# One streaming layer on one core: two buffers for the convolution's input, and all nine gather buffers for 48 tokens of tile 6

## The chip, the cores and the metric

One core of a Trainium2 chip runs the whole program in one launch. The metric is device time in microseconds (us) of an execution, as the median of several runs. A profiled execution has, beside its time, a span (from its first instruction to its last), from which every row below is taken.

## What is computed

The reference is one layer on 1024 prompt frames and 32 sample frames of width 1024. Two recurrent mixers (gated linear attention and the gated delta rule) run in chunks over a projection of the normed input; before the second mixer stands a causal convolution of width 4 over 1536 channels. Then comes a product-key expert layer (PEER), and a last norm:

```python
proj = rms_norm(x, norm_mix_w) @ w_in
conv = silu(sum(conv_in[:, i:i + l] * gdn_conv_w[i] for i in range(4)))
q2 = l2_norm(cq) * 128 ** -0.5; k2 = l2_norm(ck)
x = x + concat([o1, o2]) @ w_out
# PEER: 8 heads, 128 x 128 keys, the 16 best experts of 16384 in each head
act = gelu(einsum('thkd,td->thk', peer_u[eidx], xblk))
x = x + einsum('thk,thkd->td', gate * act, peer_v[eidx])
y = rms_norm(x, norm_final_w)
```

A token thus needs 128 rows of `peer_u` and 128 rows of `peer_v`, 4 KB each.

## The kernel before

**Tiles.** The frames lie in eight tiles of 128 (0 to 7) and the sample's tile "S" of 32. `project` (L264) makes the projection of three groups of tiles: 0, 1, S; then 2, 3, 4; then 5, 6, 7. The mixers go through the tiles in order, and the second and third projection are woven into the steps of tiles 0 to 3 (`COMING`). Behind each group of tiles come the output projection, the routing (`route`, L493) and the choice of the best experts (`select`, L832).

**The convolution.** In `project`, block u of 128 channels is made by 24 matmuls (`by_channel`, L315) into one of two PSUM banks of the stream "pv" (in the second and third projection these two alone). For the 12 blocks of the convolution the bank is copied into a tile `ci` (L383), behind three old frames (L382). The convolution is one scaled copy on ACT (L390) and three multiply-adds on DVE (L392), all of which read `ci` and make `row`; then Silu on ACT (L394), whose table is loaded ahead of it, and behind it the mixers' table again (L102). For eight blocks the squares of `row` go into a tile `sq` (L401), whose sums PE makes one block later (`norms`, L356). `ci` has one buffer, and so has `sq` in the second and third projection (in the first, `sq` lies in another pool with three).

**PEER, two ways.** Tiles 2 to 5 (`DENSE`) are computed against all 16384 experts. `gate_matrix` (L932) writes their gates to DRAM; then `dense` (L994) runs over 128 blocks of 128 experts: eight times three matmuls `pD` (L194 to L196, a product of split numbers) and Gelu; the product with the gates `w*G` (L1010); a split into two parts; and, for each four blocks, 96 matmuls `pV`, whose eight banks DVE adds to `acc` (L1039). The other tiles (0, 1, S, 6, 7) gather their rows: `u_phase` (L1084) fetches for each slot one row of `peer_u` per token by an indirect DMA from POOL into `ug` (L1098) and multiplies and sums it on DVE (L1099). `v_phase` (L1113) fetches for each token its 128 rows of `peer_v` into `vg` (L1133); after each four tokens PE sums them by eight products (`pv`, L1139). This is called a visit below; tiles 0, 1, 6, 7 have 32 visits each and S has 8, so 136.

**Buffers of the gathers.** `vg` has five; `ug` has three in one pool and one in another. In `v_phase` the flag `more` lets a token whose place in a round of nine is 5 to 8 (`own >= VB`) use a buffer of `ug`.

**Order.** A scheduler sets each engine's order from the order in which the code was written, pools' free buffers and high priority (`urgent`, L1165, gives it to each step of `v_phase`). `weave` alternates between generators step by step. At the end of the code each gathered tile's `u_phase` is woven with the `v_phase` of the tile before it, and the last tile's `v_phase` stands alone. These are written behind `dense`, so their work fills what the rest leaves. The queues themselves run strictly in the order set.

```python
    prev = None
    for t in [t for g in GROUPS for t in g if t not in DENSE]:
        weave(values(prev, False) if prev is not None else None, u_phase(t, *sel[t]))
        prev = t
    weave(values(prev, True))
```

Of the kernel before, what the change touches and what calls it, by code (L numbers as in the profile page):

```python
# [11 lines left out]
F32 = mybir.dt.float32  # L12
# [9 lines left out]
P = 128  # L22
# [13 lines left out]
GROUPS = [[0], [1, "S"], [2, 3], [4, 5], [6, 7]]  # L36

DENSE = [2, 3, 4, 5]
# [20 lines left out]
VB = 5  # L59
NG = NT + 1 - len(DENSE)  # L60
WDB = 3
EARLY = [0, 1, "S"]

SP0 = 2
# [10 lines left out]
def layer_kernel(ctx: ExitStack, tc: tile.TileContext, A: dict):  # L75
# [24 lines left out]
    def mixer_tables():  # L100

        tc.keep_in_program_order(nc.scalar.preload_act_table_set("natural_log_exp_and_others"))  # L102
# [161 lines left out]
    def project(g):  # L264
# [60 lines left out]
        def row_tile():  # L325
            return p1.tile([P, 3 * P], F32, name="row", bufs=2)
# [40 lines left out]
        for u in range(16):  # L367
            p = by_channel(A["win_c"][u])
            if len(sqs) > (1 if first and u < 12 else 0):
                norms()  # L370
            if u < 4:
                row = row_tile()
                nc.scalar.activation(row[:, :N], p[:, :N], AF.Copy, scale=0.125 if u < 2 else 1.0)
                nc.sync.dma_start(d_qk[g][:, u, :], row[:, :N])
                yield None
                continue
            b = u - 4

            nf = N - DEC if sample else N
            L = N + 3 if sample else N  # L380
            ci = p1.tile([P, 3 * P + 3], F32, name="ci", bufs=1)
            nc.vector.tensor_copy(ci[:, 0:3], hist[:, b, :])  # L382
            nc.scalar.copy(ci[:, 3:3 + nf], p[:, :nf])  # L383
            nc.vector.tensor_copy(hist[:, b, :], ci[:, nf:nf + 3])
            if sample:
                nc.vector.tensor_copy(ci[:, nf + 3:nf + 6], tails[:, b, :])
                nc.scalar.copy(ci[:, nf + 6:L + 3], p[:, nf:N])
                nc.vector.tensor_copy(tails[:, b, :], ci[:, L:L + 3])
            row = row_tile()
            nc.scalar.activation(row[:, :L], ci[:, 0:L], AF.Copy, scale=cw[:, b, 0:1])  # L390
            for i in range(1, 4):
                nc.vector.scalar_tensor_tensor(row[:, :L], ci[:, i:i + L], cw[:, b, i:i + 1], row[:, :L],  # L392
                                               op0=ALU.mult, op1=ALU.add)
            nc.scalar.activation(row[:, :L], row[:, :L], AF.Silu)  # L394

            if not first:
                mixer_tables()
            if b < 8:
                sq = (rt.tile([P, 3 * P], F32, name="sq", tag="mixT", bufs=3) if first else
                      p1.tile([P, 3 * P], F32, name="sq", bufs=1))  # L400
                nc.scalar.activation(sq[:, :L], row[:, :L], AF.Square)  # L401
                sqs.append((b, sq))
            nc.sync.dma_start(d_cv[g][:, b, 0:nf], row[:, 0:nf])
            if sample:
                nc.sync.dma_start(d_cv[g][:, b, nf:], row[:, nf + 3:L])
            yield None
# [647 lines left out]
    def idx_of(ap):  # L1054
        return bass.IndirectOffsetOnAxis(ap=ap, axis=0)
# [28 lines left out]
    def u_phase(t, ei, eiT, gate):  # L1084

        act = gs.tile([P, P], F32, name="act", bufs=2)
        h2 = ge.tile([P, D], F32, name="h2", bufs=1)
        slots = DEC if t == "S" else P
        if t == "S":
            for c in range(4):  # L1090
                nc.sync.dma_start(h2[c * DEC:(c + 1) * DEC], h2d[t])
        else:
            nc.sync.dma_start(h2, h2d[t])
        yield None
        for k in range(slots):
            e = t == 0 or k % 4 < 3
            g = (ge if e else gp).tile([P, D], F32, name="ug", bufs=UB if e else 1)
            nc.gpsimd.indirect_dma_start(out=g, out_offset=None, in_=A["u"], in_offset=idx_of(ei[:, k:k + 1]))  # L1098
            nc.vector.scalar_tensor_tensor(g, g, 1.0, h2, op0=ALU.mult, op1=ALU.mult,  # L1099
                                           accum_out=act[:, k:k + 1])  # L1100
            yield None
        with tc.high_priority():
            nc.scalar.activation(act[:, :slots], act[:, :slots], AF.Gelu_apprx_tanh)
            if t in EARLY:
                mixer_tables()
            nc.vector.tensor_tensor(act[:, :slots], act[:, :slots], gate[:, :slots], op=ALU.mult)
            wT = gs.tile([P, P], F32, name="wT", bufs=2)
            pw = bank("pw", "pv")
            by_slot(pw, act, t)
            nc.scalar.copy(wT[:, :ntok(t)], pw[:, :ntok(t)])  # L1110
        ready[t] = eiT, wT

    def v_phase(t, more):  # L1113

        eiT, wT = ready[t]
        pv = [bank("pv0", "pv"), bank("pv1", "pv")]

        ns = ntok(t) // 4
        W4 = wT[:, :ntok(t)].rearrange("p (c r) -> p c r", c=4)
        for r in range(ns):  # L1120
            wd = gp.tile([P, 4, 32], F32, name="wd", bufs=WDB)
            nc.vector.scalar_tensor_tensor(wd, bc(iota128[:, None, :32], [P, 4, 32]), float(r),
                                           bc(W4[:, :, r:r + 1], [P, 4, 32]), op0=ALU.is_equal, op1=ALU.mult)
            vs = []
            for c in range(4):
                tok = c * ns + r

                own = (r * 4 + c) % (VB + UB + 1)
                if more and own >= VB:
                    g = (ge if own < VB + UB else gp).tile([P, D], F32, name="ug", bufs=UB if own < VB + UB else 1)  # L1130
                else:
                    g = gp.tile([P, D], F32, name="vg", bufs=VB)
                nc.gpsimd.indirect_dma_start(out=g, out_offset=None, in_=A["v"],  # L1133
                                             in_offset=idx_of(eiT[:, tok:tok + 1]))
                vs.append(g)
                yield None

            def product(half, c):
                return mm(pv[half][c * 32:(c + 1) * 32, :], wd[:, c, :], vs[c][:, half * 512:(half + 1) * 512],  # L1139
                          start=(r == 0), stop=(r == ns - 1), tile_position=(0, c * 32), skip_group_check=True)  # L1140

            with tc.issue_after(product(0, 3).ins):
                for half in range(2):
                    for c in range(3 + half):
                        product(half, c)
        x = gp.tile([P, D], F32, name="xf", tag="vg", bufs=VB)
        if t == "S":
            nc.gpsimd.memset(x, 0.0)
            for c in range(4):
                nc.sync.dma_start(x[c * 32:c * 32 + ns], xdram[t][c * ns:(c + 1) * ns])  # L1150
        else:
            nc.sync.dma_start(x, xdram[t])
        for half in range(2):
            cs = slice(half * 512, (half + 1) * 512)
            nc.vector.tensor_tensor(x[:, cs], x[:, cs], pv[half], op=ALU.add)
        nf = gp.tile([P, D], F32, name="nf", tag="vg", bufs=VB)
        load_nfin(nf)
        final_norm(x, gp, nf)
        if t == "S":
            for c in range(4):  # L1160
                nc.sync.dma_start(A["ys"][c * ns:(c + 1) * ns], x[c * 32:c * 32 + ns])
        else:
            nc.sync.dma_start(A["yp"][t * P:(t + 1) * P, :], x)
# [8 lines left out]
    def some(gen, n, pace=1):  # L1172

        while n is None or n > 0:
            for _ in range(pace):
                if next(gen, 0) == 0:
                    return
            n = n and n - 1
            yield None

    def values(t, more):
        return urgent(v_phase(t, more))

    def weave(*gens):
        gens = [g for g in gens if g is not None]
        while gens:
            for g in list(gens):
                if next(g, 0) == 0:
                    gens.remove(g)
# [3 lines left out]
    p1 = p1ctx.enter_context(tc.tile_pool(name="p1", bufs=1))  # L1193
# [5 lines left out]

    lmt = mc.tile([P, 6, P], BF16, name="lmt")  # L1200
    lm0 = mc.tile([P, P], BF16, name="lm0")
    lmw = p1.tile([P, 3 * P + 3], F32, name="lmw", tag="ci", bufs=1)[:, :P]
    lmu = mc.tile([P, 8, P], U8, name="lmu")
    nc.gpsimd.memset(lmt, 1.0)
    for i in range(7):
# [28 lines left out]
    sel, picked, mixT = {}, {}, {}  # L1234
# [54 lines left out]
    gctx.close()  # L1289
    dv = ctx.enter_context(tc.tile_pool(name="dv", bufs=1, side="right", reuse_waits="tile"))  # L1290
    dense(late)
    prev = None
    for t in [t for g in GROUPS for t in g if t not in DENSE]:
        weave(values(prev, False) if prev is not None else None, u_phase(t, *sel[t]))
        prev = t
    weave(values(prev, True))


OUTS = dict(yp=(SEQ, D), ys=(DEC, D), o_gla_p=(4, 64, 128), o_gdn_p=(4, 128, 128), o_conv_p=(128, 12, 3),
# [62 lines left out]
```

## Time and profile before

| | us |
|---|---|
| runs before: median (lowest to highest of 3) | 3216.44 (3214.72 to 3219.03) |
| profiled execution: its own time | 3227.73 |
| profiled execution: span | 3226.0 |
| PE busy, share of the span | 3045.9, 94% |
| DVE busy | 2293.4, 71% |
| POOL busy | 1319.6, 41% |
| ACT busy | 1260.6, 39% |
| DMA, mean over the span | 297 GB/s |

The shares are means over stages that have different limits; the stretches are read by themselves below. The last projection runs from about 490 to 690 us, the mixers, routing and choice of experts to about 1600, `dense` from 1577 to the end with the gathers beside it. PE's busy time is modelled, since its matmuls are pipelined; DMA shares are means over 16 engines.

### The profile page before, as it was taken

The page shows a single profiled execution, that of the slowest core. Times are in us where ns is not written, and L with a number is a line of the kernel's source. Part 1 is how long each engine was busy: PE and PEld are TensorE (multiplying, and loading weights), DVE is VectorE, ACT ScalarE, POOL GpSimd, SP SyncE. Part 2 cuts the span into 40 slices and gives each one's busy share as a digit, 9 for nine tenths or more (in the row PEclk, how much of TensorE's full clock was granted, in tenths as well). Part 3 has the DMA queues.
Part 4 walks back from the last instruction along what each step waited for, and adds up shares of the span by engine and source line. Part 5 has one row for each costly group of instructions (what it writes and reads, how often), then busy time and mean ns, then how long its engine had stood idle before and what let it go on. Part 6 is the DMA issues. An engine that isn't in the chain of part 4 may idle for free.

```text
span 3226.0 us, 49510 instructions
## 1 busy us (share of the span) xinstructions
PE 3045.9 (94%) x17739; PEld 2448.0 (76%) x17739; DVE 2293.4 (71%) x5691; ACT 1260.6 (39%) x2732; POOL 1319.6 (41%) x1181
## 2 busy tenths in 40 slices
PE   7999988799999989889799999999999999999998
PEld 7899977699877877778567777777777777777664
DVE  5557378888878999999977767767677667434333
ACT  6657345535332326788623223223222223223212
POOL 2100004343244545434455555555455555333444
PEclk9989998899999999999899999999999999999999
DMA  5632568888797989999998889989899899777988
GB/s 177 178 102 94 165 212 283 267 301 304 252 333 285 336 321 356 332 337 343 343 361 327 336 330 351 344 331 365 320 354 352 319 356 342 276 269 260 355 321 303
DMA packets 363977, 959.05 MB, mean 297 GB/s; under 512 B 35745, under 2 KB 137522, under 8 KB 359634
## 3 DMA queue, kind: packets, MB, share of 16 engines
q0 software_dynamic: 156672, 570.49, 48.3%
q1 hardware_dynamic: 141266, 351.84, 30.8%
q10 hardware_dynamic: 65792, 33.56, 3.6%
q8 instruction: 139, 2.28, 0.3%
q14 instruction: 108, 0.88, 0.1%
HBM read 893.00 MB, written 62.76 MB: 296 GB/s over the span
## 4 chain that ended last, share of the span: by engine, by line
PE 48%; DVE 1%; DMA 1%; issue 0%; ACT 0%; POOL 0%; POOLq 0%; DVEq 0%
PE pD L195 7%; PE pD L194 7%; PE pD L196 7%; PE pV L194 7%; PE pV L195 7%; PE pV L196 7%; PE pv L1139 6%; DMA vg<-v,eiT 1%; DVE ug L1099 0%; DVE vl L189 0%; DVE c L887 0%; DVE xf L1052 0%; POOL vg L1133 0%; ACT rs_junk L164 0%; DVE ul L189 0%
## 5 line engine op out<-in xcount | busy, mean ns | idle before, releaser
L1098 POOL DMA_INDIRECT ug<-u,ei x544 | 651.1, 1197 | 1143.1 <-DVE ug L1099 503.1
L1133 POOL DMA_INDIRECT vg<-v,eiT x488 | 579.0, 1186 | 595.2 <-PE pv L1139 438.1
L1099 DVE SCALAR_TENSOR_TENSOR ug<-ug,h 128x1024 f32<-128x1024 f32 x544 | 658.6, 1218 | 97.3 <-DMA ug<-u,ei 91.5
L194 PE MATMUL pD<-hh,uh 128*128 128x512 f32 x1024 | 402.8, 393 | 4.8 <-ACT uh L188 4.7
L195 PE MATMUL pD<-hh,ul 128*128 128x512 f32 x1024 | 403.1, 394 | 0.4 <-DVE ul L189 0.4
L196 PE MATMUL pD<-hl,uh 128*128 128x512 f32 x1024 | 402.6, 393 | 0.0
L195 PE MATMUL pV<-vh,wl 128*128 128x512 f32 x1024 | 400.9, 394 | 0.0
L196 PE MATMUL pV<-vl,wh 128*128 128x512 f32 x1024 | 398.5, 393 | 0.0
L194 PE MATMUL pV<-vh,wh 128*128 128x512 f32 x1024 | 378.6, 394 | 5.4 <-ACT wh L188 3.9
L188 ACT CAST vh<-vx 128x1024 fp32r<-128x1024 f32 x128 | 129.3, 1047 | 564.4 <-PE pV L195 397.5
L1039 DVE TENSOR_TENSOR acc<-acc,pV 128x512 f32<-128x512 f32 x248 | 163.9, 684 | 221.8 <-PE pV L196 195.4
L189 DVE TENSOR_TENSOR wl<-w,wh 128x512 fp32r<-128x512 f32 x302 | 207.7, 689 | 104.2 <-ACT wh L188 71.1
L188 ACT CAST wh<-w 128x512 fp32r<-128x512 f32 x302 | 186.1, 618 | 229.4 <-PE pcm L321 64.2
L1139 PE MATMUL pv<-vg,wd 128*32 128x512 f32 x1952 | 263.7, 614 | 8.7 <-DMA vg<-v,eiT 7.7
L991 ACT ACTIVATE w<-pD 128x512 f32<-128x512 f32 x128 | 76.6, 598 | 497.3 <-PE pD L196 458.3
L534 PE MATMUL pq<-h2T,wqb 128*128 128x256 f32 (+2 forms) x1280 | 248.7, 347 | 2.6 <-ACT gst L960 1.0
L194 PEld LDWEIGHTS pV<-vh,wh 128*128 128x128 f32 x1024 | 192.1, 188 | 65.6 <-issue 15.9
L195 PEld LDWEIGHTS pD<-hh,ul 128*128 128x128 f32 x1024 | 192.7, 188 | 60.4 <-issue 15.9
L194 PEld LDWEIGHTS pD<-hh,uh 128*128 128x128 f32 x1024 | 192.8, 188 | 58.4 <-issue 11.6
L196 PEld LDWEIGHTS pD<-hl,uh 128*128 128x128 f32 x1024 | 192.7, 188 | 55.9 <-issue 15.9
L195 PEld LDWEIGHTS pV<-vh,wl 128*128 128x128 f32 x1024 | 193.2, 189 | 54.5 <-issue 13.4
L534 PEld LDWEIGHTS pq<-h2T,wqb 128*128 128x128 f32 x1280 | 209.8, 193 | 26.0 <-issue 3.8
(339 smaller groups left out, 5433.8 us busy)
## 6 DMA issues: line engine op xcount, KB each, us to landing
ux<-ut SPq DMA_DIRECT2D x128, 512.0 KB
vx<-v SPq DMA_DIRECT2D x128, 512.0 KB
wqb<-wq SPq DMA_DIRECT2D x80, 576.0 KB
gd<-gst ACTq DMA_DIRECT2D x16, 2048.0 KB
G<-gd SPq DMA_DIRECT2D x32, 1024.0 KB
w<-win_c SPq DMA_DIRECT2D x96, 256.0 KB
wch<-wout SPq DMA_DIRECT2D x40, 512.0 KB
w<-win_t SPq DMA_DIRECT2D x72, 256.0 KB
```

The source lines that it names most:

```text
L188: nc.scalar.copy(hi, x)
L189: nc.vector.tensor_tensor(lo, x, hi.bitcast(F32), op=ALU.subtract)
L194: mm(out, a[0], b[0], start=first, stop=False, **kw)
L195: mm(out, a[1], b[0], start=False, stop=False, **kw)
L196: mm(out, a[0], b[1], start=False, stop=last, **kw)
L534: mm(p[:, :N], w[:, kb, :], h2T[:, kb, :], start=(kb == 0), stop=(kb == KB - 1))
L991: nc.scalar.activation(w, pD, AF.Gelu_apprx_tanh)
L1039: nc.vector.tensor_tensor(acc[ti][:, cs], before[:, cs], p, op=ALU.add)
L1098: nc.gpsimd.indirect_dma_start(out=g, out_offset=None, in_=A["u"], in_offset=idx_of(ei[:, k:k + 1]))
L1099: nc.vector.scalar_tensor_tensor(g, g, 1.0, h2, op0=ALU.mult, op1=ALU.mult, accum_out=act[:, k:k + 1])
L1133: nc.gpsimd.indirect_dma_start(out=g, out_offset=None, in_=A["v"], in_offset=idx_of(eiT[:, tok:tok + 1]))
L1139: return mm(pv[half][c * 32:(c + 1) * 32, :], wd[:, c, :], vs[c][:, half * 512:(half + 1) * 512], start=(r == 0), stop=(r == ns - 1), tile ...
```

## The change

`ci` gets a second buffer, and the squares are made in the block's own `ci`, which its multiply-adds have read by then; the single `sq` of the second and third projection goes. In the first projection the squares stay where they were. At the end of the code, `more` becomes a list that `v_phase` reads anew for each token: the last tile's `u_phase` is woven with 80 steps of tile 6's `v_phase` only; then `more` is set, and the other 48 tokens of tile 6 come by all nine buffers, as tile 7's do.

```diff
+SHARE = 80
...
-            ci = p1.tile([P, 3 * P + 3], F32, name="ci", bufs=1)
+            ci = p1.tile([P, 3 * P + 3], F32, name="ci", bufs=2)
...
                 sq = (rt.tile([P, 3 * P], F32, name="sq", tag="mixT", bufs=3) if first else
-                      p1.tile([P, 3 * P], F32, name="sq", bufs=1))
+                      ci[:, :3 * P])
...
-                if more and own >= VB:
+                if more[0] and own >= VB:
...
-    prev = None
-    for t in [t for g in GROUPS for t in g if t not in DENSE]:
-        weave(values(prev, False) if prev is not None else None, u_phase(t, *sel[t]))
-        prev = t
-    weave(values(prev, True))
+    gathered, more, sums = [t for g in GROUPS for t in g if t not in DENSE], [False], None
+    for t in gathered:
+
+        weave(some(sums, SHARE) if sums and t == gathered[-1] else sums, u_phase(t, *sel[t]))
+        if t == gathered[-1]:
+            more[0] = True
+            weave(sums)
+        sums = values(t, more)
+    weave(sums)
```

The scheduler takes up both parts, and the order of all engines changes from the first convolution block on. In the three places below the lines of the new kernel are two higher than those of the old one.

**ACT, one block of the last projection.** Before:

```order
L394 ACT_TABLE_LOAD
L394 ACTIVATE row<-row 128x384
L102 ACT_TABLE_LOAD
L383 COPY ci<-pcm 128x384
L401 ACTIVATE sq<-row 128x384
L390 ACTIVATE row<-ci,cw 128x384
```

And now:

```order
L385 COPY ci<-pcm 128x384
L392 ACTIVATE row<-ci,cw 128x384
L190 CAST wh<-w 128x512
L396 ACT_TABLE_LOAD
L396 ACTIVATE row<-row 128x384
L104 ACT_TABLE_LOAD
L403 ACTIVATE ci<-row 128x384
```

The copy out of the PSUM bank stood behind the Silu of the block before it and behind both table loads; now it stands ahead of them.

**DVE, where `dense` begins** (`w*G` is the first product that `pV` needs; the tiles `c` are buffers of `select`, here of tiles 6 and 7). Before, the first `w*G`:

```order
L899 COPY_PREDICATED c_14968<-c_14969,c_14968 128x128x2
L189 TENSOR_TENSOR ul<-ux,uh 128x1024
L1010 TENSOR_TENSOR w<-w,G 128x512
L899 COPY_PREDICATED c_14968<-c_14969,c_14968 128x128
L1010 TENSOR_TENSOR w<-w,G 128x512
L189 TENSOR_TENSOR wl<-w,wh 128x512
L1063 SCALAR_TENSOR_TENSOR c_12347<-c_14969 128x128
L1064 CAST ei<-c_12347 128x128
```

And now:

```order
L1012 TENSOR_TENSOR w<-w,G 128x512 x3
L900 TENSOR_SCALAR c_15070<-c_15070 128x128
L901 COPY_PREDICATED c_15069<-c_15070,c_15069 128x128x2
L191 TENSOR_TENSOR wl<-w,wh 128x512 x2
L901 COPY_PREDICATED c_15069<-c_15070,c_15069 128x128
L191 TENSOR_TENSOR wl<-w,wh 128x512
L1012 TENSOR_TENSOR w<-w,G 128x512
L1065 SCALAR_TENSOR_TENSOR c_12332<-c_15070 128x128
L1066 CAST ei<-c_12332 128x128
L191 TENSOR_TENSOR wl<-w,wh 128x512
L1074 CAST eiT<-pe 128x128
L1041 TENSOR_TENSOR acc<-xd,pV 128x512 x4
```

Before, the first `w*G` stood while tile 6's choice ended (`c_14969`) and tile 7's was still to come; now it stands where tile 7's choice ends (`c_15070`). Counted over the whole order, 260 products of gathered rows (L1099) stood ahead of the first `w*G`, and now 273; ahead of the first `acc` 264, and now 273. On PE 33 visits and 3 of the 128 blocks of `pD` stood ahead of the first `pV`, and now 36 and 4.

**DVE at the end of the program.** Before:

```order
L1039 TENSOR_TENSOR acc<-acc,pV 128x512 x2
L1052 SCALAR_TENSOR_TENSOR acc<-acc,rs_r,nfD 128x1024
L1155 TENSOR_TENSOR xf<-xf,pv_28032 128x512
L1155 TENSOR_TENSOR xf<-xf,pv_28033 128x512
L1052 SCALAR_TENSOR_TENSOR xf<-xf,rs_r,nf 128x1024
L1353 UNCONDITIONAL_BRANCH
```

And now:

```order
L191 TENSOR_TENSOR wl<-w,wh 128x512
L1041 TENSOR_TENSOR acc<-acc,pV 128x512 x5
L1054 SCALAR_TENSOR_TENSOR acc<-acc,rs_r,nfD 128x1024 x2
L1041 TENSOR_TENSOR acc<-acc,pV 128x512 x2
L1054 SCALAR_TENSOR_TENSOR acc<-acc,rs_r,nfD 128x1024
L1041 TENSOR_TENSOR acc<-acc,pV 128x512
L1054 SCALAR_TENSOR_TENSOR acc<-acc,rs_r,nfD 128x1024
L1359 UNCONDITIONAL_BRANCH
```

The last gathered tile's end (`xf`) stood last, and now the dense tiles' (`acc`) do. On PE the last two visits stood behind the last `pV`; now 212 matmuls `pD` and `pV` stand behind the last visit. On POOL 183 gathers of `peer_v` stood behind the last one of `peer_u`, and now 187; of all 544, 56 went to a buffer of `ug`, and now 77.

## Rows read from the trace of the kernel before

**Rows 1.** part 1 of the page: busy time, share of the span, instructions of each engine

```profile
PE 3045.9 (94%) x17739; PEld 2448.0 (76%) x17739; DVE 2293.4 (71%) x5691; ACT 1260.6 (39%) x2732; POOL 1319.6 (41%) x1181
```

**Rows 2.** windows: stretch, length; busy us (instructions) by engine; granted clock; DMA share, GB/s

```profile
1500.00:1600.00 100.00, 73.63 (x398) 58.27 (x396) 97.77 (x367) 67.06 (x177) 36.09 (x29) 0.85 0.97 333
1700.00:1800.00 100.00, 99.63 (x472) 75.20 (x472) 68.34 (x103) 27.82 (x36) 53.73 (x42) 1.00 0.85 318
2800.00:2900.00 100.00, 100.00 (x488) 72.60 (x487) 38.88 (x52) 24.75 (x32) 29.44 (x30) 1.00 0.75 264
3200.00:3226.00 26.00, 11.67 (x66) 4.62 (x65) 6.60 (x7) 4.31 (x12) 2.81 (x3) 0.70 0.58 228
```

**Rows 3.** timeline of PE from 2064.7: start us, us, what; 13 dense rows left out

```profile
2064.75 0.39 PE L195 MATMUL pV<-vh,wl 128*128 128x512 f32 x1
...
2067.96 0.39 PE L196 MATMUL pV<-vl,wh 128*128 128x512 f32 x1
2068.28 1.92 PE L1139 MATMUL pv<-vg,wd 128*32 128x512 f32 x16
2070.13 0.50 PE L195 MATMUL pD<-hh,ul 128*128 128x512 f32 x1
```

**Rows 4.** tiles pD and pV: ns min/median/max, first and last start

```profile
L194 PE MATMUL pD<-hh,uh x1024: 387/389/795, 1576.8 to 3176.0; 128*128 128x512 f32 x171
L196 PE MATMUL pV<-vl,wh x1024: 387/389/632, 1597.3 to 3205.8; 128*128 128x512 f32 x171
```

**Rows 5.** timeline of POOL, tile 6 alone: first of a four of gathers

```profile
2781.84 1.30 POOL L1133 DMA_INDIRECT vg<-v,eiT  x1 [8.76 <-PE pv L1139]
...
2944.38 0.94 POOL L1133 DMA_INDIRECT vg<-v,eiT  x1 [11.13 <-PE pD L195]
```

**Rows 6.** timeline of POOL, tile 7, nine buffers: first and last of the stretch

```profile
2989.84 1.00 POOL L1133 DMA_INDIRECT ug<-v,eiT  x1 [3.87 <-PE pv L1139]
...
3204.79 0.94 POOL L1133 DMA_INDIRECT vg<-v,eiT  x1 [0.30 <-issue]
```

**Rows 7.** timeline of all engines at the end

```profile
3206.10 0.62 PE L1139 MATMUL pv<-ug,wd 128*32 128x512 f32 x1
3206.21 0.69 DVE L1039 TENSOR_TENSOR acc<-acc,pV 128x512 f32<-128x512 f32 x1 [2.06 <-issue]
...
3209.99 0.33 SPq L1045 DMA_DIRECT2D yp<-acc  x1
...
3214.71 1.03 PE L1139 MATMUL pv<-vg,wd 128*32 128x512 f32 x1 [6.68 <-DMA vg<-v,eiT]
...
3222.20 0.33 SPq L1163 DMA_DIRECT2D yp<-xf  x1
```

**Rows 8.** waits from 515 to 690: who <- for whom: us, times, longest

```profile
PE pcm L321 <- ACT ci L383: 13.3, 5, 5.1
ACT wh L188 <- DMA w<-win_t: 19.3, 5, 8.6
ACT wh L188 <- DMA w<-win_c: 15.9, 5, 7.0
```

**Rows 9.** timeline of ACT and PE around 600

```profile
598.81 1.28 ACT L394 ACT_TABLE_LOAD   x1
...
600.65 1.28 ACT L102 ACT_TABLE_LOAD   x1
601.94 0.48 ACT L383 COPY ci<-pcm 128x384 f32<-128x384 f32 x1
602.48 1.01 PE L321 MATMUL pcm<-hh,wh 128*128 128x384 f32 x2 [5.10 <-ACT ci L383]
```

**Rows 10.** windows of the last projection

```profile
520.00:600.00 80.00, 63.03 (x349) 58.52 (x347) 69.64 (x167) 47.83 (x84) 32.11 (x28) 0.88 0.85 283
600.00:690.00 90.00, 79.49 (x531) 70.02 (x531) 77.35 (x189) 45.20 (x99) 35.95 (x31) 0.87 0.84 275
```

**Rows 11.** page, costliest groups: a gathered row's product on DVE

```profile
L1099 DVE SCALAR_TENSOR_TENSOR ug<-ug,h 128x1024 f32<-128x1024 f32 x544 | 658.6, 1218 | 97.3 <-DMA ug<-u,ei 91.5
```

More of the change, by code (lines that the diff above doesn't have):

```diff
@@ L1201, in layer_kernel @@
     lm0 = mc.tile([P, P], BF16, name="lm0")
-    lmw = p1.tile([P, 3 * P + 3], F32, name="lmw", tag="ci", bufs=1)[:, :P]
+    lmw = p1.tile([P, 3 * P + 3], F32, name="lmw", tag="ci", bufs=2)[:, :P]
     lmu = mc.tile([P, 8, P], U8, name="lmu")
```

## The prediction

> **What bounds the kernel now.** I read the page's busy times first, then windows to see in which stretch which engine is full, then the timelines of PE and POOL inside these stretches, and last the waits of the stretch in which the convolution is made. By the page PE is 94% busy, DVE 71%, POOL 41%, ACT 39% [rows 1]. These are means. The windows [rows 2] show two regimes. Up to about 1600 us DVE is the full engine (97.77 of 100 us from 1500 to 1600, PE 73.63). From 1700 on PE is (99.63, then 100.00 of 100 us, at a granted clock of 1.00), while DVE falls to 39.
>
> PE's busy time is modelled, so I check it by starts. From 2064.75 to 2067.96 fourteen dense matmuls start in a row, 3.21 us, so 0.229 us each; a visit (the sixteen small matmuls for four gathered tokens) starts at 2068.28 and the next dense matmul at 2070.13, so a visit costs 2.17 − 0.23 = 1.94 us [rows 3]. `dense` has 128 blocks of 24 `pD` and 24 `pV`, 6144 matmuls in all: 1407 us. Of 136 visits 33 stand ahead of the first `pV` and two behind the last, and the other 101 take 196 us. Together that is 1603 us of the 1629 between the first `pD` at 1576.8 [rows 4] and the last dense product's end, for which I take the visit behind it at 3206.10 [rows 7]. So 26 us at most are PE's idle time in there. **A gather that lands sooner shortens nothing in this stretch.** The change can act in three places only: at the very end, in the projections, and where `dense` begins.
>
> **Term 1, the end: −8.3 us.** While tile 6 has only five buffers, POOL issues four gathers and then waits for a visit to free buffers, 8.76 or 11.13 us at a time; twelve such fours take from 2781.84 to 2944.38, so 162.5 us for 48 gathers, 3.39 us each [rows 5]. Tile 7 with nine buffers takes 1.95 us each (110 intervals from 2989.84 to 3204.79) [rows 6]. The change gives tile 6's last 48 tokens the nine buffers, so the chain of gathers should end 48 × (3.39 − 1.95) = 69 us sooner. The DMA engines have room: share 0.75 in 2800 to 2900 [rows 2]. Now see what the gathers hold up [rows 7]. The last dense product is done by 3206; a visit follows there, and the last visit starts only at 3214.71, after 6.68 us for a gather; then come the last tile's end and its output at 3222.20, and the span ends at 3226.0, with PE's clock at 0.70 in that window [rows 2]. With 69 us gained, the visits are no longer last: the new order puts 212 dense matmuls behind the last visit, 212 × 0.229 = 48.5 us, which is well inside what the gathers gain. So the end becomes: 3206.1, plus the two visits that now lie inside `dense` (2 × 1.94 = 3.9), plus the dense tail from the last product to its output's issue (3209.99 − 3206.1 = 3.9), plus the output's landing, as at the end before (3226.0 − 3222.20 = 3.8). That is 3217.7, 8.3 us less than 3226.0. Bounds: 0 if the gathers gain under about 10 us and still end last, −10 if the dense tail takes half. What is late next is PE itself.
>
> **Term 2, the convolution's input: −8 us, between 0 and −27.5.** From 515 to 690 us PE waits five times, 13.3 us in all, for ACT to copy the bank into `ci`, since both banks are full [rows 8]. The longest wait is shown by ACT's timeline [rows 9]: the copy at 601.94 stands behind two table loads of 1.28 us and a Silu, and PE's matmul at 602.48 has waited 5.10 us. With two `ci` the copy stands ahead of them in ACT's order, so these 13.3 us can go. But PE idles 17.0 us in 520 to 600 and 10.5 in 600 to 690, 27.5 in all [rows 10], and the work behind the copies is bound elsewhere too: ACT's casts of the weights wait 19.3 and 15.9 us for DMAs [rows 8], and the DMA share is 0.84. Blocks that come sooner run into these. So one end is no gain at all, the other is all of the 27.5, and I take 8, some 60% of the 13.3 that the rows name. Whether it reaches the end depends on the stretch up to 1600, in which DVE is full. The gain is kept if DVE, too, gets its inputs sooner; it is at 70 and 77 of 80 and 90 us here [rows 10], so it has only about 23 us of slack itself. The squares in `ci` cost nothing by themselves: the same activation writes the same number of elements. They do add a wait, as a `ci` comes free only when PE has summed the squares. What stands behind that is DVE's copy of the old frames (L382) and DVE's row behind it; with two buffers it comes a block later, and I put it at 0, and at +5 us for the bound (five times a matmul's 1.01 us [rows 9]). Five more table loads on ACT (6.4 us) are covered by an engine that is 39% busy [rows 1]; without that cover they would cost these 6.4.
>
> **Term 3, where `dense` begins: +3 us, between 0 and +23.** The first `acc` now has nine more gathered products ahead of it on DVE (273 for 264), at 1.218 us [rows 11] 11.0 us; against that PE has three visits (3 × 1.94 = 5.8) and a block of `pD` (24 × 0.229 = 5.5) more ahead of its first `pV`, 11.3 us of useful work that is then not done later. These cancel but for the last rows of tile 7's choice; I take +3. All of it counts on PE only if PE runs dry, which it already nearly does there (26 us idle in 1500 to 1600 [rows 2]). The upper end is the second rival below. The order of tiles 0, 1 and S is otherwise the same, and 21 more gathers to buffers of `ug` (77 for 56) cost POOL nothing, as it waits most of its time.
>
> **Sum.** −8.3 − 8 + 3 = −13.3 us. The profiled execution took 3227.73 us (its span 3226.0 and 1.73 around it), so 3214.4 by that. It lies 11.3 us above the median of the runs, 3216.44, so I give the same difference from the median: **3203.1**. With the terms' nearer bounds (−3 to −14 for the second, 0 to +8 for the third) the forecast's own range is 3195 to 3212.
>
> **Rivals.**
> *Given back (0.22).* The 13.3 us of waits are replaced by waits for weights and DVE, so the second term is 0, and the start costs +8. For it: the 35.2 us for weights [rows 8] and a full DVE to 1600 [rows 2]. Against it: PE's waits for the copy are real, and ACT casts weights sooner in the new order. 3216.44 − 8.3 + 8 = 3216.1.
>
> *Slower: the first `w*G` comes late (0.14).* In DVE's new order the first `w*G` stands where tile 7's choice ends, no longer tile 6's. 13 more products (260 to 273) are 15.9 us [rows 11], and tile 7's choice on a full DVE is about as much again, an estimate from the same stretch: 34 us. PE has 11.3 us of visits and `pD` to fill it; the rest, 23 us, is idle time ahead of the first `pV`. With no gain in the projections: −8.3 + 23 = +14.7, 3231.1. It decides if PE idles over some 15 us more between 1500 and 1660 than now. Against it: a place in the order is not a time, and DVE may reach it sooner.
>
> *All of the projection's idle time goes (0.12).* 27.5 us, and the granted clock of 0.88 and 0.87 there [rows 10] rises with PE's work. −8.3 − 27.5 + 3 = −32.8, so 3183.6.
>
> *The gathers, not PE, set the end (0.03).* Then PE has slack inside `dense`, and the chain's 69 us come off whole, or near it: 3216.44 − 69 = 3147.4. The starts speak against it: 1603 of 1629 us are accounted for by matmuls at their closest spacing. The Trainium skill (Perfetto Trace Analysis, section Identifying the Most-Contended Engine) warns that the share of time in which matmuls are busy is no good measure, since they are pipelined, and would have one look at the share of weight loads. That share is 76% here [rows 1], so by that rule a quarter of PE would be free, and this rival the forecast; the spacing of 0.229 us shows that it is not.
>
> The likeliest case, the sum above, has the remaining 0.49.
>
> **How the numbers follow.** I count 0.2%, 6.4 us, as what a measurement of this kernel can tell: faster is below 3210.0, slower above 3222.9. Faster: the third and fourth rival and most of the forecast, 0.12 + 0.03 + 0.45 = 0.60. Same: the first rival and the forecast's upper edge, 0.22 + 0.03 = 0.25. Slower: the second rival and 0.01, 0.15. The range goes from 3183 (the projection's whole gain) to 3226 (half of the late start), which leaves out the fourth rival, part of the third and most of the second, about 0.2.
>
> **What would show it.** Term 1: the last gathers of tile 6 about 1.95 us apart; the last visit some 48 us ahead of the last `pV`; the issue of `acc`'s output as the last row of the end, with no visit waiting for a DMA behind the last `pV`. Term 2: the wait of `pcm` for the copy gone between 515 and 690, and less PE idle time in its two windows; if the wait is gone and the idle time is not, the first rival holds. Term 3: the first `pD` and `pV` (1576.8 and 1597.3 [rows 4]) move earlier by the second term's gain, less 3 us. The prediction is wrong if PE idles over 15 us more in 1500 to 1660 than before, if the gathers of tile 6 don't speed up, or if `dense` from its first `pD` to its last `pV` takes anything but its 1629 us plus the two visits and what the start adds.

## The result, and the profile after

| | us |
|---|---|
| kernel before: median (4 runs; the range) | 3215.64 (3214.72 to 3219.03) |
| changed kernel: median (4 runs; the range) | 3248.31 (3239.80 to 3252.63) |
| ratio, 95% interval | 1.0093 (1.0078 to 1.0108) |
| changed kernel, profiled execution: time, span | 3239.80, 3238.1 |

The change makes the kernel 33 us slower between the medians, 12.1 us between the two profiled spans (3226.0 and 3238.1). The forecast was 3203.1, and its range ended at 3226. The profiled execution of before (3227.73) lies 12.1 us above its median, that of the changed kernel 8.5 below; a second profile of the changed kernel, below, has a span of 3249.1 and the same shape.

Part 1 of the changed kernel's page differs little from [rows 1]: no engine has much more to do.

```profile
PE 3034.5 (94%) x17739; PEld 2445.8 (76%) x17739; DVE 2290.1 (71%) x5691; ACT 1267.4 (39%) x2737; POOL 1323.4 (41%) x1181
```

Windows of the changed kernel (columns as in [rows 2]): the stretch where `dense` begins, and the end.

```profile
1500.00:1600.00 100.00, 73.67 (x406) 59.52 (x404) 88.42 (x276) 74.69 (x193) 40.81 (x32) 0.80 0.89 302
1600.00:1700.00 100.00, 70.24 (x320) 50.85 (x321) 70.82 (x156) 29.35 (x47) 50.78 (x41) 0.83 0.94 351
1700.00:1800.00 100.00, 100.00 (x475) 75.49 (x474) 68.18 (x102) 27.18 (x35) 49.57 (x41) 1.00 0.93 335
3200.00:3226.00 26.00, 26.00 (x116) 21.45 (x116) 10.18 (x14) 6.91 (x14) 0.00 (x0) 1.00 0.04 15
```

Before, for 1600 to 1700:

```profile
1600.00:1700.00 100.00, 92.38 (x413) 68.46 (x413) 76.19 (x143) 29.93 (x47) 52.72 (x43) 0.97 0.92 348
```

From 1700 on PE is full as before. **Most of the loss is in one place**: between 1600 and 1700 PE is busy for 70.24 us where it was 92.38, 22.1 us less, at a granted clock of 0.83. The waits of PE from 1500 to 1700 (who, for whom: us, times, longest), first before, then of the changed kernel, say what it waits for:

```profile
PE pw L1082 <- DVE act L1106: 11.6, 1, 11.6
PE pgm L959 <- ACT gA L956: 8.5, 10, 1.5
...
PE pV L194 <- ACT wh L188: 3.9, 2, 2.1
```

```profile
PE pgm L961 <- ACT gA L958: 24.3, 13, 8.9
PE pV L196 <- ACT wh L190: 18.8, 2, 18.6
PE pv L1141 <- DMA vg<-v,eiT: 12.0, 1, 12.0
```

`pV` waits 18.6 us for `wh`, which is cast from the first `w*G`. So the first `w*G` is late. To see why, follow it back through timelines and lists of tiles. Before, the last write of the gates to DRAM (ACT's queue), the loads of `G` and the one ahead of them (SP's), the first `w*G` (DVE) and the first `pV` (PE):

```profile
1556.28 0.52 ACTq L962 DMA_DIRECT2D gd<-gst  x1
```

```profile
1575.67 0.30 SPq L1091 DMA_DIRECT2D h<-h2d_S  x1
1576.07 1.01 SPq L1000 DMA_DIRECT2D G<-gd  x2
```

```profile
1590.03 0.67 DVE L1010 TENSOR_TENSOR w<-w,G 128x512 f32<-128x512 f32 x1
```

```profile
1596.11 1.09 PE L194 MATMUL pV<-vh,wh 128*128 128x512 f32 x4
```

And in the changed kernel:

```profile
1598.42 0.52 ACTq L964 DMA_DIRECT2D gd<-gst  x1
```

```profile
1619.69 0.80 SPq L1002 DMA_DIRECT2D G<-gd  x2
```

```profile
1631.81 1.28 DVE L1012 TENSOR_TENSOR w<-w,G 128x512 f32<-128x512 f32 x2
```

```profile
1633.20 1.22 PE L196 MATMUL pV<-vh,wh 128*128 128x512 f32 x2 [18.62 <-ACT wh L190]
```

From the write's issue to the load of `G` it is 19.8 us before and 21.3 now; from there to the first `w*G` 14.0 and 12.1. So from the last gate's write to the first `w*G` it takes 33.8 and 33.4 us: the same. What moved is the write itself, by 42.1 us, and everything behind it moved with it: the first `w*G` by 41.8, the first `pV` by 37.1 (1596.1 to 1633.2). So the choice of tile 7, which now stands between that write and the first `w*G` and which the prediction's second rival feared, costs nothing there.

The Trainium skill (DMA: Bandwidth & Descriptors, section Anatomy of one DMA) gives a transfer 2.0 us and its bytes at 436 GB/s; it fits that to another path of issue than this one. For the write's 2048 KB that would be an estimate of 6.8 us. The rows show 19.8 and 21.3 between the write's issue and the load of `G`, with the DMA engines 0.89 to 0.97 busy: a price read off the Trainium skill would miss two thirds of this. In the changed kernel the load waits for the write itself. Before, it stands behind a load of `h` on SP's queue, which comes at 1575.67; in the profile of `e2` below, with the same order there, the wait of that load is put down to a write of the gates.

The gates are late because DVE does other work first. The last `gA` (a DVE product of the gate matrices, shown by the tile's list) starts at 1551.5 before and at 1589.1 now:

```profile
L953 DVE TENSOR_TENSOR gA<-iota,gmf x128: 666/681/689, 1226.0 to 1551.5; 128x512 f32<-128x512 f32 x128
```

```profile
L955 DVE TENSOR_TENSOR gA<-iota,gmf x128: 664/680/730, 1237.1 to 1589.1; 128x512 f32<-128x512 f32 x128
```

DVE's busy time up to that start, of the gathered products alone (two records a product) and of the tiles `c` alone, on which the routing and the choice work (windows by line and by tile; behind the length, DVE's busy time is the first column of the first row, the third of the second), before and then now:

```profile
0.00:1551.50 1551.50, 307.89 (x504) 0.95 0.77 263
...
0.00:1551.50 1551.50, 0.88 (x10) 0.49 (x10) 308.23 (x1770) 49.01 (x160) 0.95 0.77 263
```

```profile
0.00:1589.10 1589.10, 323.84 (x530) 0.94 0.78 265
...
0.00:1589.10 1589.10, 0.82 (x10) 0.50 (x10) 324.06 (x1905) 55.15 (x177) 0.94 0.78 265
```

13 more products (504 to 530 records) are 15.95 us, 135 more records on `c` (22 of them the routing's, the others the choice's) 15.83: 31.8 of the 37.6 us by which the last `gA` moved. Counted over the order, 252 products stood ahead of the last `gA`, and now 265; of tile 6's choice nothing did, and now nearly all of it does. The gates stand behind them in DVE's queue. The Trainium skill (PSUM — Partial Sum Buffer, section Engine vs sequencer instructions) calls these queues strict FIFO; these rows agree.

DVE is not slower, it does its work in another order: up to 1589.1 it is busy for 1283.78 us before and 1284.23 now. What comes sooner is the last routing, and tile 6's choice behind it. The last of its products `psc` on PE starts 38.4 us earlier:

```profile
L546 PE MATMUL psc<-wqb,qb x256: 270/275/527, 416.8 to 1533.6; 128*128 128x128 f32 x128
```

```profile
L548 PE MATMUL psc<-wqb,qb x256: 273/275/377, 419.9 to 1495.2; 128*128 128x128 f32 x128
```

In the projection the wait did go, and others took its place. PE's waits from 515 to 690 now (for before [rows 8]):

```profile
PE pga L632 <- DVE kh L627: 10.0, 4, 3.8
PE pga L632 <- DVE att L642: 4.7, 3, 2.6
PE pgs L656 <- DVE mix L680: 3.8, 1, 3.8
PE pcm L323 <- ACT ci L385: 3.2, 2, 2.6
```

`pcm` waits 3.2 us for the copy where it waited 13.3. But PE then stands behind the mixer's DVE steps (`kh`, `mix`), and the last matmul of the last projection starts at 658.1, later than before (653.4):

```profile
L321 PE MATMUL pcm<-hh,wl x408: 289/337/689, 20.4 to 653.4; 128*128 128x384 f32 x90, 128*128 128x288 f32 x46
```

```profile
L323 PE MATMUL pcm<-hh,wl x408: 289/337/525, 20.5 to 658.1; 128*128 128x384 f32 x90, 128*128 128x288 f32 x46
```

PE's busy time from 500 to 700 is 165.28 us, 4.4 less than the 169.66 of before.

At the end the first term of the prediction can be read off. The last visit stands at 3180.0, ahead of the last `pV`; the last rows of DVE are `acc`:

```profile
3180.04 0.59 PE L1141 MATMUL pv<-vg,wd 128*32 128x512 f32 x1
...
3230.04 0.39 PE L198 MATMUL pV<-vl,wh 128*128 128x512 f32 x1
```

```profile
3230.46 0.69 DVE L1041 TENSOR_TENSOR acc<-acc,pV 128x512 f32<-128x512 f32 x1 [0.83 <-PE pV L198]
3232.93 1.28 DVE L1054 SCALAR_TENSOR_TENSOR acc<-acc,rs_r,nfD 128x1024 f32<-128x1024 f32 x1 [1.78 <-ACT rs_r L172]
```

From the last `pV` to the span's end it is 8.1 us (3230.0 to 3238.1); before it was 20.2 (3205.8 to 3226.0). Less the two visits that now lie inside `dense` (3.9), that is 8.2 us gained.

### The profile page after: what moved, and what is told of

It reads as the page before. It is cut to its first block, busy times and chain, and to the rows that moved or that the text cites. A ratio compares the mean times of both kernels' runs of the same rounds, so it can differ in the third digit from the quotient of the medians.

```text
span 3238.1 us, 49519 instructions
## 1 busy us (share of the span) xinstructions
PE 3034.5 (94%) x17739; PEld 2445.8 (76%) x17739; DVE 2290.1 (71%) x5691; ACT 1267.4 (39%) x2737; POOL 1323.4 (41%) x1181
## 4 chain that ended last, share of the span: by engine, by line
PE 50%; DMA 5%; DVE 4%; ACT 2%; issue 1%; POOL 0%; ACTq 0%; DVEq 0%
PE pV L196 7%; PE pV L198 7%; PE pV L197 7%; PE pD L197 7%; PE pD L198 7%; PE pD L196 7%; PE pv L1141 6%; DMA gd<-gst 5%; PE pgm L961 1%; DVE ug L1101 1%; DVE gA L955 1%; DVE gB L953 1%; ACT gA L958 1%; PE pq L536 0%; ACT gst L962 0%
## 5 line engine op out<-in xcount | busy, mean ns | idle before, releaser
L1135 POOL DMA_INDIRECT vg<-v,eiT x467 | 566.1, 1212 | 476.6 <-PE pv L1141 336.3
L1141 PE MATMUL pv<-vg,wd 128*32 128x512 f32 x1868 | 256.0, 602 | 13.8 <-DMA vg<-v,eiT 13.7
L198 PEld LDWEIGHTS pV<-vl,wh 128*128 128x128 f32 x1024 | 192.4, 188 | 54.5 <-issue 13.4
```

Source lines behind the costliest of these rows:

```text
L198: mm(out, a[0], b[1], start=False, stop=last, **kw)
```

## The experiments

Twelve experiments, four on each of three chips. The kernel before stood at 3217.67 (21 runs), 3232.33 (23) and 3230.71 us (35) on them, so ratios to its runs on the same chip are compared, not times. **Theory G** (late gates): the convolution's part changes the order, DVE does products and choice ahead of the last gate matrices, and `dense` starts late. **Rival P**: the projection itself lost the time. **Rival S**: the faster gathers disturb `dense`. Where a row is shown, it is one tile's list: times of one (min/median/max, ns), first and last start.

### First chip: the parts alone, and the gates put first

`e1_ci_only` is the kernel before with the first part of the change:

```diff
-            ci = p1.tile([P, 3 * P + 3], F32, name="ci", bufs=1)
+            ci = p1.tile([P, 3 * P + 3], F32, name="ci", bufs=2)
...
-                      p1.tile([P, 3 * P], F32, name="sq", bufs=1))
+                      ci[:, :3 * P])
```

> Only the convolution's part: two ci, squares in ci; the end of the program as before. Theory G (late gates): the whole loss comes from this part, because the order it brings puts more of DVE's other work ahead of the last gate matrix. Then the last write of the gates is issued at about 1598 us (before 1556.3), the first pV starts at 1633 within 6 us (before 1596.1), and the time is 3245 to 3258, at or a little above the changed kernel's 3248. Rival P (the projection itself lost the time, its clock being 0.83 in 600 to 700 where it was 0.89): also slow, but the first write of the gates and all after it are late by one constant amount, some 14 us, not by a growing one. Rival S (the faster gathers at the end disturb dense): this kernel is at 3216 or below.

Measured: 3244.28 us, 1.0072 (1.0051 to 1.0093).

```profile
L962 ACTq DMA_DIRECT2D gd<-gst x16: 520/521/578, 1269.1 to 1605.3; - x16
```

```profile
L194 PE MATMUL pV<-vh,wh x1024: 387/389/796, 1641.0 to 3238.5; 128*128 128x512 f32 x171
```

The loss is all here. The time is a microsecond below what was expected. Beside `e2` on the same chip (below) the first gate write is 22.6 us late (1246.5 there), the last 54.0 (1551.3): it grows, which speaks against P's constant amount as the whole cause. S falls.

`e2_share_only` is the second part alone (the diff above, without the lines on `ci` and `sq`).

> Only the end: 48 tokens of tile 6 by nine buffers; the convolution as before. Theory G: everything up to dense as before (last write of the gates 1556, first pV 1596, each within 4 us); the last visit lies ahead of the last pV, and the end saves what the prediction's first term says, 8 us: 3205 to 3211, 0.9965 to 0.9985 of before. Rival S: slower than before by 10 us or more, with dense matmuls further apart than 0.229 us where the gathers are faster.

Measured: 3212.44 us, 0.9980 (0.9966 to 0.9994), 5.2 us faster.

```profile
L964 ACTq DMA_DIRECT2D gd<-gst x16: 520/521/577, 1246.5 to 1551.3; - x16
```

```profile
L1141 PE MATMUL pv<-vg,wd x1868: 592/592/1063, 895.5 to 3177.5; 128*32 128x512 f32 x187
```

```profile
L196 PE MATMUL pV<-vh,wh x1024: 387/389/628, 1590.9 to 3203.4; 128*128 128x512 f32 x171
```

The front is that of before (5 us early), the last visit lies ahead of the last `pV`, the time is just above the range expected.

`e3_gates_first` is the whole change, and the gates in the helper `urgent`:

```diff
-    gms = chain(*(gate_matrix(t) for t in GORD[:GN]))
+    gms = urgent(chain(*(gate_matrix(t) for t in GORD[:GN])))
...
-    weave(selecting(), chain(gms, *(gate_matrix(t) for t in GORD[GN:])),
+    weave(selecting(), urgent(chain(gms, *(gate_matrix(t) for t in GORD[GN:]))),
```

> The change whole, and beside it high priority for each step of the gate matrices (the helper urgent, as v_phase has it); nothing else. Theory G: the last write of the gates comes back to 1550 to 1570, the first w*G to 1585 to 1605, the first pV to 1590 to 1610, and the time to 3200 to 3218. Rival P: the priority does not touch the projection, so the time stays above 3235. Rival S: the same, above 3235.

Measured: 3222.44 us, 1.0010 (0.9994 to 1.0026), a little above the range expected.

```profile
L964 ACTq DMA_DIRECT2D gd<-gst x16: 520/520/578, 1260.1 to 1558.8; - x16
```

```profile
L196 PE MATMUL pV<-vh,wh x1024: 387/389/504, 1602.3 to 3218.2; 128*128 128x512 f32 x171
```

With both buffers and the gates early again, `dense` begins 34 us sooner (1636.7 in the run below, on the same chip, to 1602.3) and 24 us are back. P falls as the main cause, as the convolution is still the changed one. But 10 us remain to the end alone, and the projection's own share is not nothing: its last matmul starts at 655.8 here and at 649.6 in `e2`.

`after_again` is the changed kernel once more.

> The changed kernel a second time, as its first profile explains only 12 of the 33 us between the medians. Theory G: again the last write of the gates at 1598 within 8 us and the first pV at 1633 within 8 us; 3240 to 3253. If the two executions differ by 10 us, the stretch in which they part (windows of 100 us) is to show whether it is the gates' stretch or another.

Measured: 3246.13 us, 1.0074 (1.0052 to 1.0096), span 3249.1; last gate write 1599.3, first `pV` 1636.7. Of the 11.0 us between its span and the first profile's, 3.5 are at the first `pV`; the rest comes inside `dense`, where PE waits longer for casts of `w` and `u`: its waits from 1700 on are, for `wh` and `uh`,

```profile
PE pV L196 <- ACT wh L190: 4.3, 3, 3.3
PE pD L196 <- ACT uh L190: 4.0, 2, 2.4
```

where the first profile has 1.2 and 2.6.

This run and `e2` differ in the convolution alone, on one chip. Between their profiles the last `gA` moves from 1546.1 to 1590.0, 43.9 us. Up to it DVE is busy for 1248.1 and 1284.7 us, so 36.6 of the 43.9 are work that now comes first; the other 7.3 are idle time of DVE, 6.9 of it ahead of 700, and that is what is left for P.

### Second chip: other ways to late gates

`e4_sq_only` has the squares in the block's `ci`, of which there is still one (the second pair of lines of `e1`'s diff). The other half, two `ci` beside the old `sq`, was not tried: the kernel's tiles leave no room for it.

> Before, and only the squares made in the block's ci, which keeps its one buffer. In its order 263 gathered products stand on DVE ahead of the last gate matrix (252 before, 265 with both buffers) and tile 7's whole choice ahead of the first w*G. Theory G (late gates cost the time, not the second buffer as such): the last write of the gates comes 25 to 45 us later than before's 1556, the first pV 25 to 45 later than 1596, and the time is 3235 to 3255. Theory B (the second buffer is what brings the late order): within 5 us of before, 3212 to 3222, with the gates at 1556.

Measured: 3277.21 us, 1.0140 (1.0107 to 1.0174), 45 us slower and more than expected. `e7`, whose order up to `dense` is that of before, gives the same chip's front: last gate write 1568.3, first `pV` 1608.0. Here:

```profile
L962 ACTq DMA_DIRECT2D gd<-gst x16: 520/521/4440, 1281.6 to 1628.8; - x16
```

```profile
L194 PE MATMUL pV<-vh,wh x1024: 387/389/794, 1672.1 to 3266.8; 128*128 128x512 f32 x171
```

60.5 and 64.1 us late. Theory B falls: the squares' place brings a late order without the second buffer. With a single `ci` the projection is late as well: in 515 to 690 PE waits 9.2 us for the squares it is to sum, the projection's last matmul starts at 683.5 (`e7` 650.4), and the gates' first write is 26 us late (1281.6; `e7` 1255.6). So these 45 us are not the gates' order alone.

`e6_late_gates` is the kernel before, with a lower priority for the last gates alone (`later` is `urgent` with a negative offset):

```diff
-    weave(selecting(), chain(gms, *(gate_matrix(t) for t in GORD[GN:])),
+    weave(selecting(), later(chain(gms, *(gate_matrix(t) for t in GORD[GN:])), 1500),
```

> Before, and only a lower priority for the gate matrices that are still open when the last choice begins, so that 61 more instructions of the choice and 4 more gathered products stand on DVE ahead of the last one; convolution and end as before. Theory G: the last write of the gates 12 to 25 us later than 1556, the first pV later by about as much, PE gets one block of pD and one visit done ahead of it (7.4 us), and the time goes up by what is left, 5 to 18 us: 3222 to 3236. If the gates' place does not decide, within 4 us of before.

Measured: 3257.58 us, 1.0088 (1.0064 to 1.0113).

```profile
L962 ACTq DMA_DIRECT2D gd<-gst x16: 520/521/2500, 1254.8 to 1593.1; - x16
```

```profile
L194 PE MATMUL pV<-vh,wh x1024: 387/389/793, 1636.0 to 3236.0; 128*128 128x512 f32 x171
```

This shows the last step by itself: with the old convolution and the old end, gates that are 24.8 us late (1568.3 in `e7` to 1593.1) and a first `pV` 28.0 us late (1608.0 to 1636.0) cost 25 us between the medians. Of the 24.8, 12.5 are at the last `gA` (1563.6 and 1576.1), the rest at the steps behind it, which have the lower priority too. The size is above the 5 to 18 expected: the first `pV` came later than the 12 to 25 us thought of, 28.0 less the 7.4 of work done ahead is 20.6, and 25 were measured.

`e5_share_gates` has the second part of the change and `e3`'s two lines.

> Only the end of the program (48 tokens by nine buffers) and high priority for the gate matrices; the convolution as before. The first experiment on the gates with the whole change stood 10 us above the end alone. Theory G with a gain that is given back (the two ci bring nothing to the gates): this kernel is at 3203 to 3213, at or below the end alone (3212), and 8 to 18 below the whole change with gates first (3222). Rival: the priority itself costs those 10 us by moving other work behind the gates; then this kernel is at 3217 to 3226.

Measured: 3237.24 us, 1.0021 (1.0002 to 1.0040). This missed: it is no faster than before. As a ratio it lies where the rival put it, that the priority itself costs those 10 us (3217 to 3226 is up to 1.0026 on the first chip). `e7_share_24` is the end with `SHARE = 104`.

> The end alone, with 24 tokens of tile 6 by nine buffers for 48 (SHARE 104). By the prediction's first term the gain is that the visits no longer come last, not the gathers' speed: half the tokens gain 35 us on the gathers, still more than the 15 that are wanted, so the time is that of 48 tokens, 3208 to 3216. If the gathers' own time counted, half the gain would be lost: 3215 to 3217 or, against before, 0 to -3 us.

Measured: 3235.13 us, 1.0007 (0.9989 to 1.0024). Not the gain of 48 tokens, but on another chip.

### Third chip: the end and the gates side by side

`e8_share_48`, `e9_share_24b`, `e10_share_gates_b` and `e11_whole_gates_b` are `e2`, `e7`, `e5` and `e3`.

> The end alone, 48 tokens, again, beside the next three on one chip, since the first eight runs lay on two chips, on which before stood at 3218 and at 3232. Theory G: 0.9965 to 0.999 of before, as the first time (0.998). If the gain of the first time was the chip's, 0.999 to 1.002.

> The end alone with 24 tokens, again. If only the place of the last visits counts, the same ratio as with 48 tokens, to within 0.0015. If the gathers' gain itself counts, higher than with 48 tokens by 0.002 or more.

> The end, and high priority for the gate matrices, the convolution as before; again. If the priority itself costs something, because the first w*G then stands behind 18 more instructions of the choice (1320 for 1302), this is above the end alone by 0.001 to 0.004; if not, within 0.001 of it.

> The whole change with gates first, again. Against the kernel before it in this call it has the two ci alone. If the two ci bring nothing to the end once the gates are early: within 0.0015 of it. If they bring the prediction's 8 us: 0.0025 below it. If they cost something of their own beside the gates: 0.0025 or more above it.

| | us | ratio (95%) |
|---|---|---|
| `e8`: end, 48 tokens | 3220.73 | 0.9967 (0.9951 to 0.9984) |
| `e9`: end, 24 tokens | 3225.81 | 0.9986 (0.9968 to 1.0004) |
| `e10`: end, gates first | 3232.29 | 1.0006 (0.9989 to 1.0023) |
| `e11`: whole change, gates first | 3235.17 | 1.0020 (1.0000 to 1.0040) |

The end alone gains on this chip too. 24 tokens lie between 48 and none here, and at 1.0007, no gain, on the second chip; the intervals overlap, so how much of the gain needs the second 24 stays open. In the profile of `e9` PE is held up once more, between 2920 and 2940, at a clock of 0.91:

```profile
2920.00:2940.00 20.00, 18.02 (x80) 12.70 (x79) 11.67 (x16) 10.98 (x16) 8.21 (x7) 0.91 0.94 344
```

`e10` stands 0.0039 above `e8`: the priority itself costs 11.6 us. (Not by the 18 more instructions of the choice that were expected: by the records of the traces 9 fewer of `select` stand ahead of its first `w*G` than in `e8`.) Its gates are written 4.7 us sooner than `e8`'s (1556.8 and 1561.5), and yet the first `pD` starts later, 1589.8 for 1582.0, and the first `pV` with it (1606.3 for 1602.4). The longest wait (PE's waits from 1500 to 1610):

```profile
PE pw L1084 <- DVE act L1108: 13.8, 1, 13.8
```

`pw` stands ahead of the first `pD` on PE and waits for a gathered tile's last products, which the gates were put before; it starts at 1584.9; in `e8` its wait is 11.6 and it starts at 1572.5. So with the gates early the next thing that is late is that. It explains the first `pD`; of the 8.0 us between the two spans 3.9 are at the first `pV`, and the other 4.1 come inside `dense`, from a cause that stays open. `e11` stands 0.0014 above `e10`, within the 0.0015: the two `ci` bring nothing that shows once the gates are early. The intervals leave no room for a gain of 8 us, but some for a loss of as much.

## Why the prediction was wrong

- **Term 1, the end, −8.3 us: right.** 8.2 by the profile of the changed kernel; alone, −5.2 and −10.0 us between medians on two chips. The reason was right (the last visits move into `dense`). Its supporting number was too good: from the first of tile 6's last 48 gathers (2764.74) to the first of tile 7's (2888.39) POOL takes 123.7 us, 2.6 each, not 1.95. Before, it took 160.6 (2771.64 to 2932.23), so the gathers gained 37 us, not 69, which was still enough. POOL goes on waiting for the visits that free the buffers, 7.37 us for one at 2888.39. In the whole change this gain is no help on top: in `e1` the late `dense` ends behind the last visit (3234.9) already.
- **Term 2, the convolution, −8 us: wrong, it is 0 at best.** The step that failed is from "the wait goes" to "PE gets further". The wait went (13.3 to 3.2), and the mixer's waits took its place; PE had done no more by 700, and the projection's last matmul started 4.7 us later. The rival "given back" named this, with DVE and the weights' loads for the cause; the longest waits now are on DVE, by way of the mixer.
- **Term 3, where `dense` begins, +3 us: wrong, it is about +20.** The first `pV` comes 37.1 us late; ahead of it PE has done three visits and a block of `pD` more (11.3, as the prediction priced them), and from the first `pV` to the last it then loses 5.5 us less (what is left of the last `pV`'s 24.2 us when the two more visits' 3.9 are counted). 37.1 − 11.3 − 5.5 = 20.3. With −8.2 at the end that is the profiled +12.1. The prediction asked what DVE does ahead of the first `w*G` and put tile 7's choice there; it did not ask when the gates are ready that `w*G` multiplies by. The order showed it: the last `gA` behind 13 more products and behind tile 6's choice.
- **The slower rival (0.14) had the place and the sign, and the wrong wait.** It put the first `pV` 23 us later than PE's work could fill, by 34 us of products and choice ahead of the first `w*G`; the measured 25.8 (37.1 − 11.3) came by 31.8 us of products and choice ahead of the gates. So its price was near for nearly the right work, at another place. It took no gain in the projection, as it was. Its condition, PE idling over 15 us more from 1500 to 1660, was met: busy 104.12 us for 126.01. Its +14.7 stands beside +12.1 between the two profiled spans, and beside +32.7 between the medians, as the profile of before lies 12.1 us above its median and the first of the changed kernel 8.5 below. So the sums above are those of two executions, and that +14.7 is so near +12.1 is luck; the size of the loss is the runs', 28 us on the first chip and 33 in the runs of the result. The pair on the first chip that differs in the convolution alone, `e2` and the second profile of the changed kernel, accounts for that size: the first `pV` is 45.7 us later (1590.9 to 1636.7), 34.4 without the 11.3 of work done ahead, 2.8 more come inside `dense`, and the spans differ by 37.2, the medians by 33.7.
- **The fourth rival** falls: the gathers were 38 us sooner done (last one issued at 3166.4 for 3204.8) and the time did not follow.

What stays open is why the plan puts the last routing, products and choice ahead of the gates as soon as the squares' place changes. That it does, and what it costs, is shown; which of its rules does it was not tried.

## What to carry to other kernels

Where a scheduler sets the order, a change far up the program can be priced only by what it does to the order at the next hand-over between stages: find the instruction that the next stage waits for, follow it back to its last producer, and count what stands ahead of that producer on the engine that is full. A wait that is taken from an engine which is not the bound there gives back nothing by itself. And price each part alone: here one part gains 0.2 to 0.3% and is the version to keep, the other loses more than that.

## What was not expected of the hardware

- Executions of one kernel spread more than the first runs showed: 3207.18 to 3228.87 us in 21 runs of the kernel before, where the first four lay within 4.3 us; and the same kernel's median was 14.7 us higher on the second chip.
- A wait of PE of 12.0 us is followed by slow matmuls. In the changed kernel the granted clock is 0.58 and 0.57 in the two windows in which PE hardly works, near the lower of its two levels (1.2 of 2.4 GHz), and 1.00 in the next:

```profile
1600.00:1620.00 20.00, 3.64 (x16) 0.59 (x16) 12.97 (x64) 9.66 (x21) 12.19 (x11) 0.58 1.02 359
1620.00:1640.00 20.00, 6.80 (x21) 5.22 (x22) 18.45 (x35) 4.75 (x7) 5.33 (x4) 0.57 1.00 390
1640.00:1660.00 20.00, 20.00 (x96) 15.07 (x96) 12.47 (x20) 2.11 (x2) 8.68 (x8) 1.00 0.68 229
```

The visit of the first window, which before took 1.92 us [rows 3], takes 3.64 there.
